# Layer 0 of a two-layer decoder trunk: tokens laid out by residue class, value projections as seven half-size products, blocks of the first attention group taken from the folded layout

## The chip, the cores and the metric

The kernel runs on one core of one Trainium2 chip. The metric is the device time of one execution in microseconds; the time of a kernel is the median of its runs. A core has a matrix engine (TensorE, in the profile PE, with its weight loads as PEld), two engines for elementwise work (VectorE, DVE; ScalarE, ACT), a general one (GpSimd, POOL), and a queue engine (SyncE, SP) that here only issues transfers. Each engine works through its own instructions in order and waits on semaphores for the others. Matrix products land in PSUM, of which this kernel uses eight banks of 128 x 512 float32; everything else lies in SBUF.

## What is computed

512 tokens of 1024 channels go through two layers. Layer 0 mixes tokens by attention in three groups of eight heads, layer 1 by trailing means; each is followed by a gated feed-forward block with 2816 hidden channels. Cut to what matters here:

```python
ATTN_PAIRS = ((128, 1), (512, 4), (2048, 16))     # window, dilation
qkv = (h @ w_qkv).reshape(B, S, 3, 3, 8, 128)      # group, q/k/v, head, dim
for g, (window, dil) in enumerate(ATTN_PAIRS):
    # inside each of the dil residue classes: a causal band of width window/dil
    o_g, lse_g = dilated_window_attention(q, k, v, window, dil, slopes[g])
wts = softmax(stack(lses), axis=0)                 # over the three groups
x = x + (sum(wts * outs)) @ w_out
x = x + (silu(gate) * up) @ w_down                 # after RMSNorm
```

With 512 tokens, group 1 has four residue classes of 128 tokens each; group 2 is computed in the same four classes, with all pairs masked whose distance is not a multiple of 16. Group 0 has a band of 128 tokens and is computed in four blocks of 128 queries against the block itself and the one before.

## The kernel before

All large matrices are kept as sums of two float32r parts, a high and a low one: ScalarE copies a weight tile to its high part and VectorE subtracts (`split`, L77 to L79). A product of two such matrices is three matmuls: high by high, high by low, low by high.

*Two kinds of product.* `Product` (L217 to L251) gives 128 output channels for all 512 tokens from eight chunks of 128 input channels: 24 matmuls that stream 512 columns, all recorded on L245, L246 and L248. `seven` (L393 to L431) gives two such outputs at once in seven half-size products in place of eight: 84 matmuls that stream 256 columns (L384 to L386, in `mult`). It needs the weights in three combined forms and a plain quarter, which the class `Pair` makes: three loads on SP and one accumulating load on GpSimd (L134 to L138), two additions on VectorE (L150, L151), three splits of 128 x 1024 and one of 128 x 512. The token side is combined once, in `prepare` (L661), which writes the operands `T["11"]` to `T["4"]`. The results are put together by four VectorE additions out of PSUM (L420, L424, L429, L430).

*Order of work.* `units`, `loads` and `steps` are queues in the order in which products will ask for weights; `pump` starts the next loads and splits as buffers come free. There are five split tiles of 1024 columns (`w`), two of 512 (`half`), four raw tiles (`raw`) and two raw halves.

*Layer 0.* For each head the queries and keys of the three groups are made (for head 0 and 1 by `Product`, from head 2 on by three calls of `seven`). The values are made for two heads at a time: on even heads `values` (L496 to L522) makes those of group 0 for this head and the next, with the tokens as the stationary operand, in 96 matmuls of 256 columns (L509 to L511); on odd heads `values12` (L473 to L494) makes those of groups 1 and 2 in 96 matmuls of 512 columns (L484 to L486) whose stationary operand is read with a stride of four tokens (`H[k]` rearranged by `fold`, L482), and ScalarE copies the four results out (L493).

*Layout.* Tokens are kept in their natural order. Groups 1 and 2 want them by residue class, so their queries and keys are written in class order when they leave PSUM: `Folded` (L361) for `seven`, L469 for the single products; L650 reads and writes the output through a stride of four.

*Attention of a head.* `scores0` (L530) makes the scores of group 0, `scores12` (L564) those of groups 1 and 2. A row's maximum and sum for group 0 lie in block order, those for groups 1 and 2 in class order, so each pair is sent through DRAM to the other order: `dn` (L560, L561) and `df` (L587, L588), all four issued on SP. `merge` (L591) combines maxima and sums and scales the scores, `turn` (L611) transposes them on TensorE, `output` (L629) multiplies them by the values. `between` (L737) and the dictionaries given to `values` and `values12` say after which product each of these steps is written for each head; the scheduler then orders the instructions of each engine by priority and readiness. `halve` splits a head's output into two parts for the output projection; the last steps of head 7 stand in L788 to L802.

*Start.* Five matmuls on zeros run first (`WARM`, L707), then four products with the chunks as they arrive (L709 to L724), a fifth (L725), the row factors of the norm (`rstd`, L726; `spread`, L731) amid a sixth.

Of the kernel before, what the change touches and what calls it, by code (L numbers as in the profile page):

```python
# [16 lines left out]
P = 128  # L17
S = 512
# [8 lines left out]
NT = S // P  # L27
FAR = 3.0e38
# [8 lines left out]
WARM = 5  # L37
# [11 lines left out]
def trunk(ctx: ExitStack, tc: tile.TileContext, xT, norms, w_first, w_qk, w_qkp, w_v0, w_v12, w_out, w_pair, w_down, w_pin, w_pgrp,  # L49
# [72 lines left out]
    class Pair:  # L122
# [3 lines left out]
        def __init__(self, src):  # L126
            self.src, self.w = src, {}
            loads.append((self, {"raw": 2, "rawhalf": 1}, self.load))
            steps.extend([(self, "w", self.blocks), (self, "w", self.sums), (self, "w", self.more),
                          (self, "half", self.last)])  # L130
# [43 lines left out]

    def plain_gu(layer, j):
        src = w_pair[layer, j]
        units.extend([Plain(src[:, S:3 * S]), Plain(src[:, 3 * S:], src[:, :S])])
# [4 lines left out]
    for h in range(HEADS):  # L182
        if h == 0:
            plain(*[w_qk[u] for u in range(len(QK) - NF)])
        for g in range(3):
            if h == 1 and g < NSOLO:
                plain(*[w_qk[len(QK) - NF + 2 * g + c] for c in range(2)])
            elif h:
                units.append(Pair(w_qkp[3 * h - 3 - NSOLO + g]))
        if h % 2 == 0:  # L190
            plain(*[w_v0[h // 2, i] for i in range(2)])
        else:
            plain(*[w_v12[h // 2, i] for i in range(4)])
    plain(*[w_out[m] for m in range(KC)])

    def ffn_plan(layer):
        for hf in range(2):
            for j in range(hf * HALF, (hf + 1) * HALF):
                if j < NPLAIN:
                    plain_gu(layer, j)  # L200
                else:
                    units.append(Pair(w_pair[layer, j]))
# [141 lines left out]
    class Straight:  # L344


        @staticmethod
        def both(t):
            return t.rearrange("p (a c) -> p a c", a=2)

        @classmethod
        def one(cls, t, a):
            return cls.both(t)[:, a]

        scratch = out = both

        @staticmethod
        def twice(v):
            return v[:, None].to_broadcast([P, 2, H2])

    class Folded(Straight):  # L361


        @staticmethod
        def both(t):
            return t.rearrange("p (a i r) -> p a r i", a=2, r=NT)

        @staticmethod
        def scratch(t):
            return t.rearrange("p (a r i) -> p a r i", a=2, r=NT)  # L370

        @staticmethod
        def out(t):
            return t.rearrange("p (r a i) -> p a r i", a=2, r=NT)

        @staticmethod
        def twice(v):
            return v[:, None].to_broadcast([P, 2, NT, H2 // NT])

# [13 lines left out]
    def seven(T, one, two, scratch, view=Straight, after={}):  # L393


        unit = units.popleft()
# [10 lines left out]
        nc.scalar.copy(view.scratch(first)[:, 0], view.one(p1, 0))  # L407
# [12 lines left out]
        nc.vector.tensor_add(view.out(one), view.both(p26), view.twice(view.scratch(first)[:, 0]))  # L420
# [3 lines left out]
        nc.vector.tensor_add(view.scratch(sums), view.both(p73), view.twice(view.out(one)[:, 1]))  # L424
# [4 lines left out]
        nc.vector.tensor_sub(view.out(two), view.both(p45), view.twice(view.scratch(sums)[:, 0]))  # L429
        nc.vector.tensor_sub(view.out(one)[:, 1], view.scratch(sums)[:, 1], view.one(p45, 1))  # L430
# [19 lines left out]
    fold = "p (i r) -> p r i"  # L450
    unfold = "p (r i) -> p r i"


    with tc.tile_pool(name="opool", bufs=1) as opool:
        early = opool.tile([P, HEADS, S], F32R, tag="o", name="early")
        with tc.tile_pool(name="apool", bufs=1) as apool:
# [5 lines left out]

            def evac(h, u, p):
                g, c = QK[u]
                t = apool.tile([P, S], F32, name=f"qk{g}{c}")
                if g == 0:
                    nc.vector.tensor_mul(t, p, rows["row"])
                else:
                    nc.vector.tensor_mul(t.rearrange(unfold, r=4), p.rearrange(fold, r=4),  # L469
                                         rows["row"].rearrange(fold, r=4))  # L470
                QKV[h, g, c] = t

            def values12(after={}):  # L473
# [3 lines left out]
                ps4 = [ps() for b in range(NT)]  # L477
                for k in range(KC):
                    if k % 2 == 0:
                        w = weights()  # L480
                    wh, wl = (v[:, k % 2 * S:(k % 2 + 1) * S] for v in w.t)
                    oph, opl = (v.rearrange(fold, r=4) for v in H[k])  # L482
                    for b in range(NT):
                        nc.tensor.matmul(ps4[b], oph[:, b, :], wh, start=k == 0, stop=False)  # L484
                        nc.tensor.matmul(ps4[b], oph[:, b, :], wl, start=False, stop=False)  # L485
                        nc.tensor.matmul(ps4[b], opl[:, b, :], wh, start=False, stop=k == KC - 1)  # L486
                    if k % 2:
                        w.done()
                    pump()
                    for f in after.get(k, ()):  # L490
                        f()
                for b in range(NT):
                    nc.scalar.activation(t[:, b, :], ps4[b], AF.Copy)  # L493
                return t  # L494

            def values(of, r=None, after={}):  # L496


                w = weights(), weights()
                t = apool.tile([P, NT, 2 * P], F32, name="v0")  # L500
                for b in range(NT):
                    if b % 2 == 0:
                        p = ps()
                    o = blk(p, b % 2 * 2, 2)
                    for k in range(KC):
                        c = slice(k % 4 * 2 * P, (k % 4 + 1) * 2 * P)
                        wh, wl = (v[:, c] for v in w[k // 4].t)
                        mh, ml = (blk(v, b) for v in of(k))
                        nc.tensor.matmul(o, mh, wh, start=k == 0, stop=False)  # L509
                        nc.tensor.matmul(o, mh, wl, start=False, stop=False)  # L510
                        nc.tensor.matmul(o, ml, wh, start=False, stop=k == KC - 1)  # L511
                    if b % 2:
                        for a in (b - 1, b):
                            nc.scalar.activation(t[:, a, :], blk(p, a % 2 * 2, 2), AF.Copy,
                                                 scale=r[:, a:a + 1] if r is not None else 1.0)
                    pump()
                    for f in after.get(b, ()):
                        f()
                for v in w:
                    v.done()  # L520
                pump(2)
                return t  # L522
# [7 lines left out]
            def scores0(h):  # L530
# [28 lines left out]
                with nc.allow_non_contiguous_dma(reason="a few numbers a token"):  # L559
                    nc.sync.dma_start(dn.rearrange("s (b p) -> p s b", p=P), st[:, 0, 0])  # L560
                    nc.sync.dma_start(st[:, 1, 1], dn.rearrange("s (i r) -> i s r", r=4))  # L561
                A[h] = dict(b12=b12, st=st, nm=nm, s0=s0)

            def scores12(h):  # L564
# [21 lines left out]
                with nc.allow_non_contiguous_dma(reason="a few numbers a token"):  # L586
                    nc.sync.dma_start(df.rearrange("s (i r) -> i s r", r=4), st[:, 0, 1])  # L587
                    nc.sync.dma_start(st[:, 1, 0], df.rearrange("s (b p) -> p s b", p=P))  # L588
                A[h]["s12"] = s12

            def merge(h):  # L591
# [6 lines left out]
                nc.vector.tensor_max(mx, st[:, 0, :, 0, :], st[:, 1, :, 0, :])  # L598
# [30 lines left out]
            def output(h):  # L629
# [13 lines left out]
                nc.scalar.copy(o0, po)  # L643
# [457 lines left out]
```

## Time and profile before

| | |
|---|---|
| median of three runs | 1275.57 us (1275.15 to 1278.36) |
| the profiled execution | 1277.5 us, of which the span of instructions is 1275.7 us |
| TensorE busy | 1262.7 us, 99% of the span |
| VectorE busy | 866.3 us, 68% |
| ScalarE busy | 529.4 us, 41% |
| GpSimd busy | 106.4 us, 8% |
| read from HBM | 160.40 MB, 127 GB/s over the span |

Layer 0's attention lies in the first 517 us of the span, layer 0's feed-forward block from there to about 868 us, the trailing means of layer 1 up to about 930 us, and its feed-forward block after that. How to read the views: a group of instructions is given as line, engine, operation, written tile and read tiles, how many there are, their busy time and the mean of one, and what ended the idle time before them. A matmul's recorded duration contains its way through the array, which overlaps the next one; what a matmul costs in a stream is the distance from its start to the next start. A window is a stretch of the span with the busy time of each engine in it and, in brackets, the number of instructions.

### The profile page before, as it was taken

To read this page: it belongs to the slowest core of one execution; us is meant where nothing else is said; L and a number is where in the kernel's file an instruction comes from. 1 tells how busy PE (TensorE), PEld (TensorE's weight loads), DVE (VectorE), ACT (ScalarE), POOL (GpSimd) and SP (SyncE) were. 2 spreads that over 40 slices of the span, in tenths; PEclk is the share of its full clock that TensorE was granted. 3 is DMA by queue.
4 is the path that set the end of the run, shared out by engine and by line. 5 is a ranking of instruction groups with operands and counts; after the bars stand their busy time and mean duration, and the time that the engine had idled before them with its cause. 6 is when DMAs were issued, how large, how long until landed. Compare 5 with 4: busy or idle time off the path is not lost.

```text
span 1275.7 us, 20125 instructions
## 1 busy us (share of the span) xinstructions
PE 1262.7 (99%) x8036; PEld 1165.3 (91%) x8036; DVE 866.3 (68%) x1313; ACT 529.4 (41%) x825; POOL 106.4 (8%) x105
## 2 busy tenths in 40 slices
PE   9999999999999999999999999999999999999997
PEld 7989999999999998889989999888788988999986
DVE  6794876658566637578636887458978853788643
ACT  6443444444344424445324454333443532455331
POOL 1101101010110100001001110000300000111000
PEclk9999999999999999999999999999999999999999
DMA  8143546446644713147346774333124645676222
GB/s 292 52 142 75 149 133 137 124 110 159 119 117 134 179 53 124 58 100 183 121 141 156 187 180 126 108 139 116 50 67 111 173 139 132 173 182 170 95 69 66
DMA packets 83454, 163.88 MB, mean 128 GB/s; under 512 B 27440, under 2 KB 29504, under 8 KB 83360
## 3 DMA queue, kind: packets, MB, share of 16 engines
q1 hardware_dynamic: 67792, 132.82, 33.4%
q0 software_dynamic: 14416, 28.72, 13.5%
q8 instruction: 63, 1.03, 0.3%
q10 hardware_dynamic: 1152, 1.05, 0.2%
q14 instruction: 31, 0.25, 0.1%
HBM read 160.40 MB, written 2.16 MB: 127 GB/s over the span
## 4 chain that ended last, share of the span: by engine, by line
PE 80%; issue 10%; DVE 6%; DMA 2%; ACT 1%; POOL 1%; SPq 0%; DVEq 0%; POOLq 0%; ACTq 0%
PE ps L385 12%; PE ps L384 12%; PE ps L386 12%; PE ps L245 9%; PE ps L248 9%; PE ps L246 9%; PE ps L484 2%; PE ps L485 2%; PE ps L486 2%; DVE wlo L79 2%; PE ps L647 1%; PE ps L510 1%; PE ps L509 1%; PE ps L511 1%; PE ps L573 1%
## 5 line engine op out<-in xcount | busy, mean ns | idle before, releaser
L79 DVE TENSOR_TENSOR wlo<-raw,whi 128x1024 fp32r<-128x1024 f32 (+2 forms) x286 | 327.0, 1146 | 199.9 <-ACT whi L78 198.8
L78 ACT ACTIVATE whi<-raw 128x1024 fp32r<-128x1024 f32 (+2 forms) x286 | 283.9, 998 | 420.8 <-PE ps L246 203.0
L245 PE MATMUL ps<-a,whi 128*128 128x512 f32 (+1 forms) x374 | 141.0, 377 | 0.0
L246 PE MATMUL ps<-a,whi 128*128 128x512 f32 (+1 forms) x374 | 140.9, 377 | 0.0
L248 PE MATMUL ps<-a,wlo 128*128 128x512 f32 (+1 forms) x374 | 140.8, 377 | 0.0
L384 PE MATMUL ps<-tt,whi 128*128 128x256 f32 x384 | 108.7, 283 | 0.0
L385 PE MATMUL ps<-tt,whi 128*128 128x256 f32 x384 | 108.7, 283 | 0.0
L386 PE MATMUL ps<-tt,wlo 128*128 128x256 f32 x384 | 108.7, 283 | 0.0
L248 PEld LDWEIGHTS ps<-a,wlo 128*128 128x128 f32 x374 | 70.4, 188 | 12.9
L246 PEld LDWEIGHTS ps<-a,whi 128*128 128x128 f32 x374 | 70.4, 188 | 12.8
L245 PEld LDWEIGHTS ps<-a,whi 128*128 128x128 f32 x374 | 70.4, 188 | 12.7
L137 POOL DMA_DIRECT2D raw<-w_pair x32 | 38.3, 1197 | 445.7 <-DVE wlo L79 168.2
L384 PEld LDWEIGHTS ps<-tt,whi 128*128 128x128 f32 x384 | 73.7, 192 | 0.0
L385 PEld LDWEIGHTS ps<-tt,whi 128*128 128x128 f32 x384 | 73.7, 192 | 0.0
L386 PEld LDWEIGHTS ps<-tt,wlo 128*128 128x128 f32 x384 | 73.7, 192 | 0.0
L385 PE MATMUL ps<-tb,whi 128*128 128x256 f32 x256 | 72.6, 284 | 0.5 <-DVE tb L79 0.5
L386 PE MATMUL ps<-tb,wlo 128*128 128x256 f32 x256 | 72.4, 283 | 0.0
L384 PE MATMUL ps<-tb,whi 128*128 128x256 f32 x256 | 72.4, 283 | 0.0
L245 PE MATMUL ps<-h,whi 128*128 128x512 f32 x160 | 62.7, 392 | 0.0
L248 PE MATMUL ps<-h,wlo 128*128 128x512 f32 x160 | 62.3, 389 | 0.0
L246 PE MATMUL ps<-h,whi 128*128 128x512 f32 x160 | 62.3, 389 | 0.0
L384 PE MATMUL ps<-h,whi 128*128 128x256 f32 x216 | 61.9, 286 | 0.0
(247 smaller groups left out, 3329.7 us busy)
## 6 DMA issues: line engine op xcount, KB each, us to landing
raw<-w_pair SPq DMA_DIRECT2D x76, 512.0 KB, 4.2
raw<-w_qkp SPq DMA_DIRECT2D x36, 512.0 KB, 4.7
raw<-w_pair POOLq DMA_DIRECT2D x32, 512.0 KB, 7.1
raw<-w_v SPq DMA_DIRECT2D x24, 512.0 KB, 3.5
raw<-w_down SPq DMA_DIRECT2D x32, 384.0 KB, 3.1
raw<-w_down SPq DMA_DIRECT2D x32, 320.0 KB, 2.8
raw<-w_qkp POOLq DMA_DIRECT2D x18, 512.0 KB, 7.3
rawhalf<-w_pair SPq DMA_DIRECT2D x32, 256.0 KB, 3.3
```

The lines of the kernel that those rows point to most:

```text
L78: nc.scalar.activation(hi, v, AF.Copy)
L79: nc.vector.tensor_tensor(lo, v, hi.bitcast(F32), op=OP.subtract)
L137: nc.gpsimd.dma_start(self.b.t.rearrange("p (a c) -> p a c", a=2), self.src[:, None, 3 * S:].to_broadcast([P, 2, S]), accum_op=OP.add)
L245: nc.tensor.matmul(self.p[:, cols], w[0][:, s], mh[:, cols], start=self.done == 0, stop=False)
L246: nc.tensor.matmul(self.p[:, cols], w[0][:, s], ml[:, cols], start=False, stop=False)
L248: nc.tensor.matmul(self.p[:, cols], w[1][:, s], mh[:, cols], start=False, stop=self.done == self.n)
L384: nc.tensor.matmul(dst, w.t[0][:, c], th, start=k == 0, stop=False)
L385: nc.tensor.matmul(dst, w.t[0][:, c], tl, start=False, stop=False)
L386: nc.tensor.matmul(dst, w.t[1][:, c], th, start=False, stop=k == K2 - 1)
L484: nc.tensor.matmul(ps4[b], oph[:, b, :], wh, start=k == 0, stop=False)
L485: nc.tensor.matmul(ps4[b], oph[:, b, :], wl, start=False, stop=False)
L486: nc.tensor.matmul(ps4[b], opl[:, b, :], wh, start=False, stop=k == KC - 1)
```

## The change

The tokens of layer 0 are sent in by residue class from the host: position (r, i, b) of the new order is token 128 b + 4 i + r. A class of 128 tokens is then contiguous, and a block of 128 tokens is every fourth position. The change has these parts:

- `values12` becomes seven half-size products with the tokens as the stationary operand, each over two classes: 7 x 2 x 4 x 3 = 168 matmuls of 256 columns. Its weights come as two `Pair`s whose steps alternate (`pairs`). The results are put together by seven VectorE operations; the four ScalarE copies of L493 go, one ScalarE copy of the first product comes.
- The values of group 0 are made like queries and keys, with the channels on the partitions: for head 0 by two `Product`s, for heads 2, 4 and 6 by `seven` with a `Pair`; the new `turn_values` transposes them, eight transposes and two ScalarE copies for two heads, for heads 2, 4 and 6 after the next head's first `seven`.
- `Straight` and `Folded` go. Groups 1 and 2 are written as they come. Group 0's queries, keys and values are written by blocks (`by_block`): four neighbouring positions of the source go to four places 128 columns apart. `output` writes its first half through a stride of four (`block`) and adds the second without one.
- `merge` is tied by `issue_after` to the last result (`mark`) of the latest `seven` or `values12`, and moves: for odd heads h-1 it is written after the next head's first `seven`, for even ones after the second, for head 7 after `values12`. `scores0` and `turn` move with it; `scores12` goes to the first of the seven products. The two exchanges through DRAM change sides: `dn` is now written in pieces of four numbers and read in single ones, `df` written in single ones and read in fours.
- The identity and the two distance tables are loaded on SP after the first sixteen loads, not on GpSimd at the start. There are six matmuls on zeros. The fifth product is written after the first `prepare`, and all four `prepare` calls come within head 0.
- At the end of layer 0's feed-forward block `unfold` adds the last projection to the stream and writes the sum in the natural order into another tile; one ScalarE copy moves the first of these tiles back.

```diff
-WARM = 5
+WARM = 6
...
+    def by_block(t):
+        return t.rearrange("p (b a j) -> p a j b", a=2, b=NT)
+    def by_class(t):
+        return t.rearrange("p (a j b) -> p a j b", a=2, b=NT)
...
-        nc.vector.tensor_add(view.out(one), view.both(p26), view.twice(view.scratch(first)[:, 0]))
+        nc.vector.tensor_add(into(one), out(p26), again(out(first)[:, 0]))
...
-        nc.vector.tensor_sub(view.out(one)[:, 1], view.scratch(sums)[:, 1], view.one(p45, 1))
+        mark.append(nc.vector.tensor_sub(into(one)[:, 1], out(sums)[:, 1], out(p45)[:, 1]))
...
             def values12(after={}):
...
+                    for a in range(2):
+                        for k in range(K2):
+                            wh, wl = (v[:, half * S + k % 2 * H2:half * S + (k % 2 + 1) * H2]
+                                      for v in part(unit[k // 2], name).t)
+                            mh, ml = (blk(v, a) for v in T[key, k])
+                            o = both(p)[:, a]
+                            nc.tensor.matmul(o, mh, wh, start=k == 0, stop=False)
+                            nc.tensor.matmul(o, mh, wl, start=False, stop=False)
+                            nc.tensor.matmul(o, ml, wh, start=False, stop=k == K2 - 1)
...
+            def turn_values(h):
+                t = apool.tile([P, NT, 2 * P], F32, name="v0")
+                for c in range(2):
+                    p = ps()
+                    for b in range(NT):
+                        nc.tensor.transpose(blk(p, b), blk(VT[c], b), ident)
+                    nc.scalar.copy(t[:, :, c * P:(c + 1) * P], p.rearrange("p (b d) -> p b d", b=NT))
...
-                    nc.sync.dma_start(dn.rearrange("s (b p) -> p s b", p=P), st[:, 0, 0])
-                    nc.sync.dma_start(st[:, 1, 1], dn.rearrange("s (i r) -> i s r", r=4))
+                    nc.sync.dma_start(dn.rearrange("s (p b) -> p s b", b=NT), st[:, 0, 0])
+                    nc.sync.dma_start(st[:, 1, 1], dn.rearrange("s (r p) -> p s r", r=NT))
...
-                nc.vector.tensor_max(mx, st[:, 0, :, 0, :], st[:, 1, :, 0, :])
+                with tc.issue_after(mark[-1].ins) if mark else nullcontext():
+                    nc.vector.tensor_max(mx, st[:, 0, :, 0, :], st[:, 1, :, 0, :])
...
                 if h % 2:
-                    if h == 1:
-                        return {0: [], 1: [later(merge, 0)], 2: [later(turn, 0), later(scores0, 1)]}[g]
-                    return {0: [later(merge, h - 1)], 1: [later(turn, h - 1), later(scores0, h)], 2: []}[g]
-                return {0: [later(output, h - 2), later(turn, h - 1)], 1: [later(output, h - 1), later(scores0, h)],
-                        2: []}[g]
+                    return {0: [later(turn_values, h - 1)] if h > 1 else [], 1: [later(merge, h - 1)],
+                            2: [later(turn, h - 1), later(scores0, h)] + [later(scores12, h)] * (h == HEADS - 1)}[g]
+                return {0: [later(merge, h - 1), later(output, h - 2)], 1: [later(turn, h - 1), later(scores0, h)],
+                        2: [later(output, h - 1)]}[g]
...
+        def unfold(m, p):
+            if m == 0:
+                held["x", 0], t = slot("xs", F32)
+                new = t[:, 0]
+            else:
+                new = x_tile(m - 1)
+            nc.vector.tensor_add(new.rearrange("p (b i r) -> p r i b", r=NT, b=NT), *(
+                t.rearrange("p (r i b) -> p r i b", r=NT, b=NT) for t in (X[m], p)))
+            X[m] = new
```

252 lines of the change are left out of this document (132 added, 120 removed).

## The prediction

> **What bounds the kernel now.** I read the page's totals first, then what TensorE waited for, then windows over one pair of heads.
>
> ```profile
> span 1275.7 us, 20125 instructions
> PE 1262.7 (99%) x8036; PEld 1165.3 (91%) x8036; DVE 866.3 (68%) x1313; ACT 529.4 (41%) x825; POOL 106.4 (8%) x105
> ```
>
> TensorE is busy for 99% of the span. Its waits, from the longest to the last listed:
>
> ```profile
> PE ps L322 <- POOL rcol L314: 1.3, 2, 1.1
> ...
> PE ps L618 <- DVE s L606: 0.2, 1, 0.2
> ```
>
> The whole list has eight entries and none is above 1.3 us, so no other engine holds TensorE up: only fewer or cheaper matmuls shorten the span, and only a new wait of TensorE lengthens it. Two pairs of heads, and a stretch of the feed-forward block that holds nothing but half-size products (columns: window, its length, then busy time and instructions of PE, PEld, DVE, ACT and POOL, granted clock, DMA share, GB/s):
>
> ```profile
> 147.62:259.05 111.43, 111.43 (x835) 111.03 (x835) 73.67 (x118) 45.74 (x84) 12.56 (x13) 1.00 0.52 132
> 259.05:370.49 111.44, 111.44 (x836) 111.05 (x835) 73.16 (x118) 45.56 (x84) 12.33 (x13) 1.00 0.58 129
> 710.00:750.00 40.00, 40.00 (x336) 40.00 (x335) 34.55 (x48) 20.96 (x28) 4.61 (x4) 1.00 0.74 183
> ```
>
> A pair of heads costs 111.4 us, all of it TensorE; VectorE works for 66% of that. The third row gives the price of a 256-column matmul, 40.00 / 336 = 0.119 us, and shows TensorE unhindered beside a VectorE that is 34.55 / 40.00 = 86% busy. The granted clock is full throughout.
>
> **The change part by part.** *`values12`.* The old call for head 3, from its first matmul to the first of the next product:
>
> ```profile
> 205.73 0.51 PE L484 MATMUL ps<-whi,h 128*128 128x512 f32 x1
> ...
> 211.49 1.95 PE L573 MATMUL ps<-qk,qk 128*128 128x128 f32 x16
> 213.19 0.60 PE L484 MATMUL ps<-whi,h 128*128 128x512 f32 x1
> ...
> 230.42 0.28 PE L384 MATMUL ps<-h,whi 128*128 128x256 f32 x1
> 230.54 0.28 PE L385 MATMUL ps<-h,whi 128*128 128x256 f32 x1
> ```
>
> From 205.73 to 230.42 are 24.69 us; 213.19 - 211.49 = 1.70 of them are the scores of L573. So 96 matmuls cost 22.99 us, 0.239 each. The new call has 168 of 256 columns. The last two rows stand 0.12 apart, the window gave 0.119; at 0.1195 the call costs 20.1 and saves 2.9 us, four calls 11.6. This does not ask why the old call paid 0.239; the stride of its stationary tiles is only the likeliest reason. The Trainium skill ("TensorE: Matmul & The Clock Gate", section "Back-to-back issue gap") lists 518 cycles for 512 columns and 262 for 256 at 2.4 GHz, by which I estimate 96 x 0.216 = 20.7 us before and 168 x 0.109 = 18.3 after: 2.4 saved a call, 9.6 in four, or 2.0 less than by the rows. No stream of either width here is that fast, so the rows stand.
>
> *`values`.* The eight transposes of `turn_values` are priced by the eight of `turn`:
>
> ```profile
> 133.28 0.87 PE ps L624 x8
> ```
>
> For heads 2, 4 and 6, 96 matmuls become 84: 12 x 0.1195 = 1.43 saved, 0.87 paid, 0.56 left, 1.7 in three. For head 0 they become 48 of 512 columns, at the distance of these rows:
>
> ```profile
> 42.45 0.39 PE L246 MATMUL ps<-early,whi 128*128 128x512 f32 x1
> 42.68 0.39 PE L248 MATMUL ps<-early,wlo 128*128 128x512 f32 x1
> 42.91 0.28 PE L509 MATMUL ps<-whi,early 128*128 128x256 f32 x1
> 43.02 0.28 PE L510 MATMUL ps<-wlo,early 128*128 128x256 f32 x1
> ```
>
> 48 x 0.23 + 0.87 - 96 x 0.1195 = 0.4 us lost.
>
> *The sixth matmul on zeros.*
>
> ```profile
> 1.24 4.63 PE L708 MATMUL ps<-idle 128*128 128x256 f32 x10 [1.24 <-DVE idle L705]
> 6.41 0.79 PE L245 MATMUL ps<-early,whi 128*128 128x512 f32 x1 [0.54 <-ACT whi L718]
> ...
> 9.99 0.55 PE L248 MATMUL ps<-early,wlo 128*128 128x512 f32 x1
> 10.38 0.39 PE L245 MATMUL ps<-early,whi 128*128 128x512 f32 x1
> 10.61 0.40 PE L246 MATMUL ps<-early,whi 128*128 128x512 f32 x1
> ```
>
> One more is 4.63 / 5 = 0.93 us; 0.54 of it fits into the wait for the first weights, so the loss is 0.4, at most 0.9. Matmuls of 512 columns stand 0.39 apart until 10.38 and 0.23 after it. Should that switch come earlier by as much as TensorE starts earlier, up to 1.6 would be gained. I take the loss of 0.4.
>
> *VectorE.* The rows of its work (out and in shapes, count, busy time and mean ns, idle time before):
>
> ```profile
> L79 DVE TENSOR_TENSOR wlo<-raw,whi 128x1024 fp32r<-128x1024 f32 x222 | 270.3, 1220 | 131.4 <-ACT whi L78 131.0
> L150 DVE TENSOR_TENSOR raw<-raw 128x512 f32<-128x512 f32 x50 | 34.2, 684 | 16.7 <-issue 16.4
> L420 DVE TENSOR_TENSOR qk<-ps,first 128x512 f32<-128x512 f32 x18 | 12.3, 683 | 0.0
> L430 DVE TENSOR_TENSOR qk<-sums,ps 128x256 f32<-128x256 f32 x18 | 7.4, 409 | 0.0
> L467 DVE TENSOR_TENSOR qk<-ps,row 128x512 f32<-128x512 f32 x4 | 2.6, 680 | 1.1 <-ACT row L731 1.1
> L469 DVE TENSOR_TENSOR qk<-ps,row 128x512 f32<-128x512 f32 x8 | 8.3, 1068 | 0.0
> L650 DVE TENSOR_TENSOR o<-o,ps 128x512 f32<-128x512 f32 x8 | 8.9, 1107 | 14.9 <-PE ps L647 14.9
> ```
>
> A `Pair` takes 3 x 1.22 + 3 x 0.68 = 5.7 us (two additions, one half split). For `values12` two of them replace four plain splits: 11.4 - 4.9 = 6.5 more, and seven results of 0.68 add 4.8. For `values` one replaces two splits, 3.3 more, and four results add 3 x 0.68 + 0.41 = 2.5. L650 without its stride gives back 2 x 0.4. That is 16.3 a pair of heads. Writing by blocks is new. L469 reads the row factors from SBUF, and its product from PSUM, through a stride: 0.39 over L467. L420 read PSUM through the same stride at 683, so the dearer part is SBUF. L650 also writes through one and costs only 0.04 more than L469. So a block-wise write lies between nothing and 0.4 us; over the results of three products, 3 x 3.5 full-size operations, at most 4.2 a pair. I take 2. VectorE then has 73.7 + 16.3 + 2 = 92.0 us in 111.4 - 2.9 - 0.6 = 107.9, or 85%, no more than the 86% beside which TensorE ran unhindered above. Without that cover each microsecond over would count in full. ScalarE, at 46 of 111 us, loses four copies and gets five smaller jobs; it is nowhere near.
>
> *Order and transfers.* `merge` waits on VectorE for both exchanges; behind it stand splits, behind those TensorE.
>
> ```profile
> 218.06 0.49 ACT L584 ACTIVATE s<-s,nm 128x256 f32<-128x256 f32 x1
> ...
> 227.39 0.17 DVE L598 TENSOR_TENSOR mx<-st 128x8 f32<-128x8 f32 x1 [5.74 <-DMA st<-df]
> ```
> ```profile
> DVE mx L598 <- DMA st<-df: 26.9, 7, 10.4
> ```
> ```profile
> dn<-st SPq DMA_DIRECT2D x8, 4.0 KB, 10.3
> st<-dn SPq DMA_DIRECT2D x8, 4.0 KB, 3.5
> df<-st SPq DMA_DIRECT2D x8, 4.0 KB, 4.3
> st<-df SPq DMA_DIRECT2D x8, 4.0 KB, 2.8
> ```
>
> The new `df` is written in single numbers, as `dn` was: 10.3 + 3.5 = 13.8 us. For an odd head h-1 it starts after the values' first product (84 / 7 = 12 matmuls, 1.4 us) or, after `values12`, its first 24 (2.9 us), and the scores: these began at 211.49 and their last exponential ended at 218.55, 7.1 us. So for an even head h, whose `values` runs, it lands near 1.4 + 7.1 + 13.8 = 22.3; for an odd head near 23.8. The new `merge` waits for the next head's first result (odd: 20.1 + 1.7 + 10.0 = 31.8) or for an even head's successor's second (later still). So it finds its data some 8 us old, and VectorE's 26.9 us of waiting should go; TensorE did not notice them, so I book nothing. SP, too, works in order, and its read of `df` cannot start before those 10.3 us are over, so the weight loads issued after it start so much later. What hides that are tiles already split: five in the ring, each good for 24 matmuls or 2.9 us, 14.3 us when full. Four raw tiles lie ahead of these. I book nothing, and at most 0.5 a head, 3.5 in seven.
>
> *Moved loads and the start.* The identity and the two tables leave GpSimd for SP, behind the first sixteen loads and ahead of the weights:
>
> ```profile
> 11.90 2.19 SPq L114 DMA_DIRECT2D raw<-w_qk x2
> ...
> 36.81 1.04 POOL L314 TENSOR_TENSOR rcol<-var,nhalf 128x4 f32<-128x4 f32 x1 [28.75 <-DVE var L312]
> ```
>
> SP issues these weights 1.1 us apart, so three loads push them back by some 3 us, while TensorE is fed from the first sixteen; and the identity is asked for only after the row factor at 36.81, some 20 us past its landing. GpSimd, which builds the bias tables from the two distance tables, has 28.75 us idle to do it in. Nothing for this; were TensorE to ask for those weights at once, the 3 us would count, but the four lead products, 96 matmuls, come first.
>
> *Head 0.* Here VectorE is the tight engine:
>
> ```profile
> 48.66:92.88 44.22, 44.01 (x234) 37.51 (x233) 39.48 (x70) 23.24 (x45) 4.47 (x5) 1.00 0.30 89
> ```
>
> It is busy for 39.48 / 44.22 = 89% already. Two `prepare` calls move ahead of this stretch's splits, the two value tiles are written by blocks, and `turn_values` asks for the second as soon as the product is done, with only the scores' 1.7 us between them. I book 1.0 (0 to 2.5), and 0.5 (0 to 1.5) for TensorE's other waits on a result within the pairs.
>
> *The tail.* `merge` of head 7 now follows `values12`; ahead of the transposes that need it TensorE has 18 matmuls of 512 columns, 18 x 0.23 = 4.1 us, and `output` of head 6. I book nothing; what is left over falls under the other waits above. `unfold` makes eight additions with a stride on both sides, by L650 against L903 at most 0.4 us dearer each:
>
> ```profile
> L903 DVE TENSOR_TENSOR x<-x,ps 128x512 f32<-128x512 f32 x30 | 20.6, 686 | 44.2 <-PE ps L248 44.2
> ```
>
> VectorE waited 44.2 us for TensorE at this line, which hides them; uncovered they would be 3.
>
> *The sum.* -11.6 - 1.7 + 0.4 + 0.4 + 1.0 + 0.5 = -11.0, so a span of 1264.7. The profiled execution took 1277.5, 1.8 over its span and 1.9 over the median of the runs: 1264.7 + 1.8 - 1.9 = 1264.6.
>
> **The rivals.** *Head 0 stalls.* The two `prepare` calls stand ahead of the splits of head 1's weights. Were all of the stage's free VectorE time, 44.22 - 39.48 = 4.7 us, to come as a wait instead, the end would be at 1264.6 + 4.7 = 1269. For it: the 89%. Against it: TensorE was busy for 44.01 of the 44.22 beside that load.
>
> *Block-wise writes are dear.* VectorE has 107.9 - 90.0 = 17.9 us left a pair before such writes; from 17.9 / 10.5 = 1.7 us more each it is the bound, and at 2.0 more a pair takes its old 111 us: near 1275, no change. Against it: no stride in the rows costs more than 0.42. The Trainium skill ("SBUF — State Buffer", the row "Cachelines" of its table) says that each step to another 16-byte line pays; by that the 16-byte stride of L469 pays at every element as a longer one would, and the price stays near 0.4. The trace bears it out as far as L467 and L469 go; no row of it has the longer stride.
>
> *Slower: VectorE stands still at `merge`.* Tied to a result, with `df` now the slow exchange and its read behind weight loads on SP, `merge` can keep the splits waiting as long as the longest wait before, 10.4 us. Of five split tiles one is being read and one written, and beside a VectorE at 85% half the ring, 7.2 us, is a fair cover: 3.2 us a head, seven heads, 22: 1287. It decides from 7.2 + 11 / 7 = 8.8 us a head. For it: the 10.4 itself. Against it: the 8 us of margin above.
>
> *It does not do what it says.* With tokens as the stationary operand and weights streaming, 256 columns could cost more than 0.1195. At 22.99 / 168 = 0.137 the main term is gone: 1264.6 + 11.6 = 1276. Against it: L509 and L510 above are of that kind, and stand 0.11 apart.
>
> **How the numbers follow.** Forecast 0.60, head 0 0.15, dear writes 0.09, `merge` 0.14, the last 0.02. The forecast's own range: the warm-up's bounds (-2.0 to +0.5 about its term), those of `turn_values` (-1.0 to +1.5) and of the other waits (-0.5 to +1.0) give 1261.1 to 1267.6 if all fall to one side. The range takes in head 0 and the edge of the third case, 1260 to 1275.5, and leaves out `merge`. A measurement tells 0.3%, 3.8 us, from no change: the first two cases are faster, 0.75; dear writes and the last are the same, 0.11; `merge` is slower, 0.14.
>
> **What would show it.** Right: matmuls of the new `values12` 0.12 apart, a call of 20 us without its scores, a pair of heads near 108 us, VectorE near 85% in it, next to no time in front of L598's successor, block-wise results at 0.7 to 1.1 us. Wrong: TensorE's waits on split tiles inside the pairs; a wait of several microseconds at `merge`; block-wise results above 2 us; a gap in front of the transposes of head 0.

## The result and the profile after

| | before | changed |
|---|---|---|
| median | 1276.70 us (10 runs, 1275.15 to 1284.85) | 1289.99 us (10 runs, 1285.53 to 1300.50) |
| ratio | | 1.0107, 95% interval 1.0080 to 1.0134 |
| profiled execution | 1277.5 us, span 1275.7 | 1300.5 us, span 1298.7 |

The change makes the kernel 1.1% slower; 1264.6 was forecast, and 1275.5 was the upper end of the range. The profiled execution of the changed kernel is the longest of its ten, 10.5 us above their median, so its waits are read for where they lie, and sizes are taken from the medians of runs. The loss lies in the attention of layer 0: VectorE's first addition of the output projection starts at 501.4 us in the profile, at 477.1 before, and what follows takes 797.3 us of span against 798.6.

The totals of the changed kernel's page:

```profile
PE 1261.7 (97%) x8274; PEld 1157.6 (89%) x8274; DVE 930.1 (72%) x1398; ACT 542.4 (42%) x831; POOL 125.5 (10%) x113
```

TensorE is no longer busy all the time: it had 99% of the span and has 97%. The pair of heads from the scores of head 3 to those of head 5, of the changed kernel, with the columns of the windows shown before:

```profile
205.50:324.83 119.33, 112.29 (x905) 110.06 (x903) 91.04 (x143) 48.76 (x86) 18.00 (x15) 0.98 0.58 140
```

A pair took 111.43 us, should have taken 107.9, and takes 119.33. VectorE has 91.04 us of work in it, where 92.0 were forecast: the load is right, the time is not. Of the 11.4 us over the forecast, 7.0 are time in which TensorE stands idle; the other 4.4 are longer busy time, at a mean granted clock of 0.98 (third number from the right). What TensorE waits for in the changed kernel (total, times, longest):

```profile
PE ps L640 <- DVE s L628: 12.4, 6, 3.3
PE ps L256 <- ACT oh L79: 5.7, 1, 5.7
PE ps L569 <- DVE qk L414: 5.1, 4, 1.5
```

L640 is the first transposition of `turn`, L628 the multiplications in `merge`; L569 is the second half of `scores0`, which waits for L414, the first result of a `seven` that VectorE reads out of PSUM, presumably for its bank; L256 is the output projection, waiting for the last heads' halves at the end of the attention. Only the first was in the list before, with 0.2 us. `merge` itself, however, no longer waits for its transfers. VectorE's waits of the changed kernel:

```profile
DVE raw L152 <- issue: 39.0, 11, 4.8
...
DVE mx L620 <- DMA st<-df: 0.6, 1, 0.6
```

The 26.9 us in front of `merge` (now L620) are down to 0.6, as forecast. Grown is L152, the first addition that makes the third form of a `Pair`'s weights (L150 before): 39.0 us in eleven waits against 16.4 in five. Between 92 and 500 us, in the attention, it is 25.1 us in six waits, one ahead of each `merge` of heads 1 to 6, against 1.4 in one before; most of the rest lies in the feed-forward blocks, where the kernel before had it too. One of the six, on VectorE of the changed kernel, ahead of the `merge` of head 4:

```profile
306.49 0.68 DVE L414 TENSOR_TENSOR qk<-ps,first 128x512 f32<-128x512 f32 x1
311.50 0.69 DVE L152 TENSOR_TENSOR raw<-raw 128x512 f32<-128x512 f32 x1 [4.33 <-issue]
312.11 0.68 DVE L418 TENSOR_TENSOR sums<-ps,qk 128x512 f32<-128x512 f32 x1
315.37 1.23 DVE L80 TENSOR_TENSOR wlo<-raw,whi 128x1024 fp32r<-128x1024 f32 x1 [2.58 <-ACT whi L79]
316.51 0.68 DVE L423 TENSOR_TENSOR qk<-ps,sums 128x512 f32<-128x512 f32 x1
317.12 0.41 DVE L424 TENSOR_TENSOR qk<-sums,ps 128x256 f32<-128x256 f32 x1
317.44 0.16 DVE L620 TENSOR_TENSOR mx<-st 128x8 f32<-128x8 f32 x1
...
321.57 1.07 DVE L628 TENSOR_SCALAR s<-s,co 128x256 f32<-128x256 f32 x4
```

and what TensorE and GpSimd did at that time:

```profile
308.44 0.28 PE L374 MATMUL ps<-h,whi 128*128 128x256 f32 x1
...
321.98 1.35 PE L640 MATMUL ps<-ident,s 128*128 128x128 f32 x7 [3.30 <-DVE s L628]
```
```profile
300.82 1.24 POOL L139 DMA_DIRECT2D raw<-w_v  x1 [17.17 <-DVE qk L424]
```

TensorE ended the `seven` whose results these are at 308.44, where the next one starts. VectorE, which works in order, has L152 ahead of the second result; L152 reads a raw tile to which GpSimd's accumulating load of 300.82 adds a quarter; that load landed 10.6 us after its issue, at 311.42, and L152 starts at 311.50. Then a split waits another 2.58. The last result, the one that `merge` is tied to, ends at 317.53, 9.1 us after TensorE was done; `merge` starts at 317.44, its first multiplications, with steps on weights in between, at 321.57, and `turn`, which TensorE reaches one product later, waits 3.30 us for them.

### The profile page after: what moved, and what is told of

It is laid out like the page before. It is cut to its first block, busy times and chain, and to the rows that moved or that the text cites. A ratio compares the mean times of both kernels' runs of the same rounds, so it can differ in the third digit from the quotient of the medians.

```text
span 1298.7 us, 20811 instructions
## 1 busy us (share of the span) xinstructions
PE 1261.7 (97%) x8274; PEld 1157.6 (89%) x8274; DVE 930.1 (72%) x1398; ACT 542.4 (42%) x831; POOL 125.5 (10%) x113
## 4 chain that ended last, share of the span: by engine, by line
PE 68%; issue 12%; DVE 10%; DMA 7%; ACT 1%; POOL 1%; SPq 0%; DVEq 0%; POOLq 0%; ACTq 0%
PE ps L256 10%; PE ps L257 10%; PE ps L374 10%; PE ps L259 10%; PE ps L375 10%; PE ps L376 10%; DMA raw<-w_qkp 3%; DVE wlo L80 2%; DMA df<-st 2%; DMA raw<-w_v 1%; PE ps L594 1%; DMA raw<-w_out 1%; ACT whi L79 1%; PE ps L669 1%; POOL rcol L325 1%
## 5 line engine op out<-in xcount | busy, mean ns | idle before, releaser
L79 ACT ACTIVATE whi<-raw 128x1024 fp32r<-128x1024 f32 (+2 forms) x297 | 294.1, 1000 | 472.1 <-PE ps L257 195.5
L80 DVE TENSOR_TENSOR wlo<-raw,whi 128x1024 fp32r<-128x1024 f32 (+2 forms) x297 | 340.3, 1150 | 176.9 <-ACT whi L79 173.7
L256 PE MATMUL ps<-a,whi 128*128 128x512 f32 (+1 forms) x374 | 141.0, 377 | 0.0
L257 PEld LDWEIGHTS ps<-a,whi 128*128 128x128 f32 x374 | 70.4, 188 | 12.8
L256 PEld LDWEIGHTS ps<-a,whi 128*128 128x128 f32 x374 | 70.4, 188 | 12.8
L374 PE MATMUL ps<-h,whi 128*128 128x256 f32 x252 | 74.0, 294 | 0.8 <-DVE sums L418 0.8
L375 PE MATMUL ps<-h,whi 128*128 128x256 f32 x252 | 72.6, 288 | 0.0
L376 PE MATMUL ps<-h,wlo 128*128 128x256 f32 x252 | 72.6, 288 | 0.0
L152 DVE TENSOR_TENSOR raw<-raw 128x512 f32<-128x512 f32 x61 | 41.8, 685 | 39.3 <-issue 39.0
```

Source lines behind the costliest of these rows:

```text
L79: nc.scalar.activation(hi, v, AF.Copy)
L80: nc.vector.tensor_tensor(lo, v, hi.bitcast(F32), op=OP.subtract)
L152: nc.vector.tensor_add(a[:, :S], a[:, :S], b[:, :S])
L256: nc.tensor.matmul(self.p[:, cols], w[0][:, s], mh[:, cols], start=self.done == 0, stop=False)
L257: nc.tensor.matmul(self.p[:, cols], w[0][:, s], ml[:, cols], start=False, stop=False)
L374: nc.tensor.matmul(dst, w.t[0][:, c], th, start=k == 0, stop=False)
```

## Experiments

Theory A, formed from the above: the loads of the values' new `Pair`s come late, VectorE stands at L152, the results and the `merge` tied to them stand behind it, and TensorE runs into `turn` and `scores0`. Theory B: one product between the last result and `turn` is too short for `merge`, loads or no loads. Medians are given with the ratio to the kernel before on the same chip, whose own median drifted from 1277.8 to 1280.7 us between the sets. Kernels are therefore compared by ratio, from 1.0107 for the changed kernel, and a hundredth stands for 12.8 us.

### The exchange, the pin and the place of `merge`

Faster `df` (e1):

```diff
-nc.sync.dma_start(df.rearrange("s (r p) -> p s r", r=NT), st[:, 0, 1])
-nc.sync.dma_start(st[:, 1, 0], df.rearrange("s (p b) -> p s b", b=NT))
+nc.sync.dma_start(df.rearrange("s (p r) -> p s r", r=NT), st[:, 0, 1])
+[nc.sync.dma_start(st[r * NI:(r + 1) * NI, 1, 0, s], df.rearrange("s (j b r) -> s r j b", b=NT, r=NT)[s, r])
+ for s in range(2) for r in range(NT)]
```

> Only the exchange df differs: written in runs of four numbers, read in single ones by eight small reads (L608, L609); the order of instructions on VectorE and TensorE stays that of the changed kernel. Theory A (the slow write keeps SP at the read of df for 11.5 us a head, the loads of the next pair of weights start late, VectorE stands at the addition L152 with the results and merge behind it): SP's wait at L609 falls from 92.0 us to under 45, VectorE's at L152 from 39.0 to under 20, TensorE's at L640 from 12.4 to under 4 and at L256 for oh from 5.7 to under 1; time 1264 to 1272. Theory B (one product between the last result and turn is too short for merge, whatever the loads do): L640 stays at 9 or more, time 1283 to 1290.

Measured: 1279.75 us, ratio 1.0017 (0.9999 to 1.0036). SP's waits of the changed kernel and then of e1:

```profile
SPq L609 <- DMA df<-st: 92.0, 8, 13.7
```
```profile
SPq L609 <- DMA df<-st: 40.2, 8, 7.7
```

and, in e1, VectorE's at the addition and TensorE's at `turn`:

```profile
DVE raw L152 <- issue: 41.4, 11, 5.3
```
```profile
PE ps L640 <- DVE s L628: 6.4, 4, 2.1
```

0.0090 are gained, some 11 us, and the wait at `turn` is halved, but neither theory is met: L152 stands as long as before. That doesn't clear SP's stand at `df`, for SP is hardly free sooner in e1. SP's rows for head 4, of the changed kernel and then of e1:

```profile
283.40 0.38 SPq L608 DMA_DIRECT2D df<-st  x1
294.54 0.38 SPq L609 DMA_DIRECT2D st<-df  x1
295.02 1.67 SPq L136 DMA_DIRECT2D raw<-w_v  x1
```
```profile
278.47 0.38 SPq L608 DMA_DIRECT2D df<-st  x1
286.07 6.21 SPq L609 DMA_DIRECT2D st<-df  x8
292.39 0.52 SPq L136 DMA_DIRECT2D raw<-w_v  x1
```

The write lands sooner, but the eight small reads take SP 6.2 us to issue. From the issue of the write to the next load of weights pass 11.6 us in the changed kernel and 13.9 in e1 here, and 13.1 and 12.4 on the mean of heads 0 to 6. So e1 does not test what it was made for, and where its 11 us come from stays open.

No pin (e2), and no pin with the faster `df` (e3):

```diff
-with tc.issue_after(mark[-1].ins) if mark else nullcontext():
+if True:
     nc.vector.tensor_max(mx, st[:, 0, :, 0, :], st[:, 1, :, 0, :])
```

> issue_after is taken away, merge may stand in VectorE's queue ahead of the results; nothing else. Theory A: the late loads stay, so the waits at L569 for the results (5.1 us) and the tail's 5.7 stay and only those at L640 shrink: 1277 to 1284. Theory B: the waits of TensorE at L640 go with the pin, 1268 to 1276. If VectorE standing at merge for the exchange were the cost that the pin avoids, slower than the changed kernel: over 1292.

> The faster exchange df and no pin. Without the pin VectorE stood 68.6 us at merge for the exchange in twelve and more microseconds each; with 8 us less a head about 15 are left. If this stand is all that the pin avoids: 1268 to 1276, level with or better than the pin. If the order of the queue itself is bad: over 1282.

Measured: 1308.89 us, ratio 1.0238 (1.0209 to 1.0268), and 1281.63, 1.0014 (0.9988 to 1.0040). The scheduler now puts `merge` ahead of results, and VectorE waits there, in e2 and then in e3:

```profile
DVE mx L620 <- DMA st<-df: 68.6, 8, 11.5
```
```profile
DVE mx L620 <- DMA st<-df: 20.7, 6, 6.4
```

In e2 VectorE stands at `merge` as in the slower rival of the prediction, which the pin avoids in the changed kernel. With the faster exchange the pin no longer matters: e3, whose time lies between the two that were expected, and e1 are alike. And yet e2 and e3 have no more than 0.3 us at L152 between 92 and 500 us, where the changed kernel has 25.1 and e1 26.5. So the stand at the addition is not the only one that costs: without it VectorE stands elsewhere in front of results, and TensorE waits 7.3 us at L569 in e3.

`merge` one product earlier (e4), and both this and the faster `df` (e5):

```diff
 # odd h
-0: [later(turn_values, h - 1)] if h > 1 else [], 1: [later(merge, h - 1)],
+0: ([later(turn_values, h - 1)] if h > 1 else []) + [later(merge, h - 1)], 1: [],
 # even h
-0: [later(merge, h - 1), later(output, h - 2)],
+0: [later(output, h - 2)],
 # odd h, h < 7
-values12({0: [later(scores12, h)]})
+values12({0: [later(scores12, h)], 6: [later(merge, h)]})
```

> merge is written one product earlier for every head but the last (for odd heads after values12, for even ones after the next head's first seven), the pin stays. Theory A: L640 falls under 4 us, the waits for results at L569 and the tail stay: 1276 to 1283. Theory B: nearly all of the loss goes, 1266 to 1273.

> Both edits, the faster df and merge one product earlier. Theory A: no better than the faster df alone within 3 us, 1263 to 1271. Theory B: as merge earlier alone, 1266 to 1273. If each cures a part of its own, 1262 to 1267, clearly below either.

Measured: 1283.60 us, 1.0029 (1.0010 to 1.0049), and 1270.51, 0.9935 (0.9911 to 0.9958). In e4 `turn` is off the list, and the other waits have grown:

```profile
PE ps L256 <- ACT oh L79: 9.2, 1, 9.2
PE ps L569 <- DVE qk L414: 7.1, 4, 2.8
```

Merge earlier gains 0.0078, the faster exchange 0.0090, both 0.0172: each cures a part of its own, and together they beat the kernel before, though not down to the 1262 to 1267 us expected of that. B explains its part, but not all. The order matters for L152 too: between 92 and 500 us its waits are 5.3 us in e4 and 5.4 in e5.

### The values' pairs

`values12` as it was, on the new layout (e6):

```diff
-pairs(w_v12[h // 2, 0], w_v12[h // 2, 1])
+plain(*[w_v12[h // 2, i] for i in range(4)])
...
+oph, opl = H[k]
+for b in range(NT):
+    nc.tensor.matmul(ps4[b], blk(oph, b), wh, start=k == 0, stop=False)
...
```

> The changed kernel with values12 as it was: four plain split tiles a call, 96 matmuls of 512 columns, four copies on ScalarE; the tokens stay by residue class, so the stationary tiles are contiguous. On TensorE 96 x 0.227 = 21.8 us a call in place of 20.1, 6.6 more in four calls, if the stride was what made 22.99; 22.99 and 11.5 more if it was not. Theory A in its present form (VectorE stands at L152 for the accumulating load of a pair, and two pairs at once for values12 fill the four raw tiles, so that loads start late): the waits at L152 in front of merge shrink for the even heads' stages, L640 falls under 8, time 1284 to 1290, the matmuls' loss nearly balanced. If pairs for values12 have no part in the waits: 1296 or more.

Measured: 1268.98 us, 0.9922 (0.9891 to 0.9952), 0.0185 or 24 us less than the changed kernel, though TensorE has more to do. I had expected the matmuls' loss to be nearly balanced. The window of e6 from the scores of head 3 to those of head 5:

```profile
200.56:310.33 109.77, 109.77 (x832) 105.66 (x831) 80.76 (x127) 48.98 (x85) 14.72 (x13) 1.00 0.57 138
```

TensorE is never idle in it. VectorE at the same place as in the section above:

```profile
296.66 0.68 DVE L414 TENSOR_TENSOR qk<-ps,first 128x512 f32<-128x512 f32 x1
297.45 0.69 DVE L418 TENSOR_TENSOR sums<-ps,qk 128x512 f32<-128x512 f32 x1
298.40 1.22 DVE L80 TENSOR_TENSOR wlo<-raw,whi 128x1024 fp32r<-128x1024 f32 x1 [0.26 <-ACT whi L79]
...
300.14 0.41 DVE L424 TENSOR_TENSOR qk<-sums,ps 128x256 f32<-128x256 f32 x1
300.47 0.16 DVE L580 TENSOR_TENSOR mx<-st 128x8 f32<-128x8 f32 x1
```

No addition stands between the results. The last of them ends at 300.55, 1.9 us after TensorE ended the product (298.62), where it was 9.1 in the changed kernel; `merge` starts at 300.47 and its multiplications at 302.45, 2.0 us later in place of 4.1. The slow exchange, the pin and the late place of `merge` are all still there in e6, and so is SP's stand at the exchange (L569 of e6):

```profile
SPq L569 <- DMA df<-st: 79.7, 8, 11.6
```

The other way round, e8 makes the two edits of e5 on e6:

> values12 plain, the faster df, and merge one product earlier. If the slow exchange and the late merge cost nothing by themselves and only turned the pairs' late loads into waits of TensorE: the same as values12 plain alone, 1267 to 1271, though these two edits took 19.5 us off the changed kernel. If they cost something of their own: under 1265.

Measured: 1270.35 us, 0.9924 (0.9895 to 0.9953), the same as e6. The two edits that were worth 0.0172 beside the pairs are worth nothing without them. In e8 VectorE even stands 16.8 us at `merge` for the exchange, and TensorE waits for nothing of it.

What about the pairs costs so much? They bring VectorE work, a load chain (a load on SP, then an accumulating one on GpSimd into the same tile), and they hold all four raw tiles, since two pairs of two are under way at once. And `values12` in seven products has its results put together on VectorE, in order with everything else there, where e6 has ScalarE copy them. VectorE's work alone, added to e6 (e11):

```diff
+spin = scratch("first")
+nc.vector.memset(spin, 0.0)
 for k in range(KC):
+    for i in range(2):
+        nc.vector.tensor_add(spin, spin, spin)
```

> values12 plain with four raw tiles, and sixteen additions of 128 x 512 on a spare tile in each call (16 x 0.68 = 10.9 us), about the work that the two pairs and the seven results add on VectorE (11.3 us). If VectorE's load is what the pairs cost: 1280 or more, with TensorE waiting for VectorE. If it is the loads and the order of the queue: within 4 us of 1269.

Measured: 1271.11 us, 0.9926 (0.9902 to 0.9951). The same pair of heads in e11:

```profile
201.93:311.69 109.76, 109.76 (x832) 105.67 (x831) 90.63 (x144) 48.74 (x85) 13.52 (x13) 1.00 0.57 136
```

VectorE is as loaded as in the changed kernel, 90.63 us against 91.04, and TensorE does not feel it. These additions wait for nothing, so e11 clears the work, not the order in which the seven results stand.

The accumulating load left out for the values' weights of the changed kernel (e9):

```diff
-nc.gpsimd.dma_start(self.b.t.rearrange("p (a c) -> p a c", a=2),
-                    self.src[:, None, 3 * S:].to_broadcast([P, 2, S]), accum_op=OP.add)
+if self.add:
+    nc.gpsimd.dma_start(...)
```

> The changed kernel without the accumulating loads of GpSimd for the weights of the values (11 of 61): one quarter of those weights is left out of the sums, so the values differ; matmuls and VectorE's work are the same. If it is this load that VectorE waits for at L152 ahead of results and merge: L152's 39.0 us fall under 20, TensorE's waits at L640 from 12.4 to under 5, time 1276 to 1283. If it is the first loads on SP or the ring of raw tiles: L152 stays over 30 and the time within 4 us of 1290.

Measured: 1280.92 us, 1.0014 (0.9992 to 1.0036). That gains 0.0093, 12 us. The addition's wait (one line further down in e9) falls, and `turn` is off TensorE's list, though its wait at the output projection is 7.8 us (5.7 in the changed kernel):

```profile
DVE raw L153 <- issue: 25.9, 7, 4.4
```

It was expected under 20. Between 92 and 500 us, where the values' weights are loaded, it fell from 25.1 to 9.7; the rest lies in the feed-forward blocks, whose loads are as before.

Late loads without pairs for `values12`: e6 with three raw tiles in place of four (e10).

```diff
-BUFS = {"w": 5, "half": 2, "raw": 4, "rawhalf": 2}
+BUFS = {"w": 5, "half": 2, "raw": 3, "rawhalf": 2}
```

> values12 plain again (1268.98 us with four raw tiles), and now three raw tiles in place of four, so that weights are loaded later while matmuls and VectorE's work stay. If late loads are what makes VectorE stand at L152 in front of results and merge: TensorE's waits at the transposes and for results come back, several us in sum, time over 1276. If the kernel has loads to spare: within 3 us of 1269.

Measured: 1296.55 us, 1.0138 (1.0104 to 1.0173). This holds for the whole kernel; the pair of heads in e10 shows the attention's part:

```profile
202.50:320.20 117.70, 113.38 (x833) 108.21 (x832) 82.44 (x131) 47.69 (x85) 13.24 (x13) 0.97 0.54 132
```

117.70 in place of 109.77: one raw tile less costs a pair of heads 7.9 us, with the same matmuls and hardly more work on VectorE (82.44 us against 80.76). But the waits at the transposes that were expected did not come back: in this window TensorE waits 3.0 us for a result at L414 and 1.3 for others. So a shortage of raw tiles costs time, but not at the transposes, where the changed kernel waits most. The opposite, a fifth raw tile for the changed kernel, was not tried.

### The start

Five matmuls on zeros in place of six, on e5 (e7) and on e6 (e12).

```diff
-WARM = 6
+WARM = 5
```

> Faster df, merge one product earlier, and five matmuls on zeros in place of six. If the sixth brings the full granted clock to the first real matmuls: 1.5 to 2.5 slower than with six, 1272 to 1273, and the first products' matmuls 0.39 apart until about 10 us. If it only costs its own length: 0.5 faster, 1270.

> values12 plain with five matmuls on zeros. If the sixth brings the full clock forward: 1 to 2 us slower than 1268.98; if it costs 0.4: 1268.5.

Measured: 1268.98 us, 0.9916 (0.9886 to 0.9947) against 0.9935 with six, and 1270.90, 0.9919 (0.9891 to 0.9948) against 0.9922. The sixth matmul can't be told from nothing in either.

## Why the prediction was wrong

*The step that failed* is the one on order and transfers, which booked nothing for `merge` and the late loads. It put the new `merge` at "20.1 + 1.7 + 10.0 = 31.8", the moment at which TensorE ends the product, and took the results as there at once. They stand in VectorE's queue, and there L152 came first: the last was 9.1 us late in the stretch shown. The same step asked of late weights only whether TensorE would run out of split tiles ("What hides that are tiles already split"). No wait for weights is among TensorE's waits of the changed kernel; what ran late was what stood behind the weights in VectorE's queue: results, `merge`, and through them, it seems, PSUM banks. That `merge` has only one more product's time, 10 us, to be done before `turn` was nowhere priced. "0.5 (0 to 1.5) for TensorE's other waits on a result within the pairs" is the term that was to hold all this. The measured time is 25.4 us above the forecast; e6 against the changed kernel puts what `values12` in seven products brings along at 24 us, and 7 more for the matmuls that e6 pays besides. Some 5 us of these 31 were gained elsewhere against the forecast, which was not traced.

*The term for `values12`* had its matmuls right and lacked its weights. The new call of head 3 on TensorE:

```profile
207.61 0.36 PE L484 MATMUL ps<-whi,h 128*128 128x256 f32 x1
...
210.57 1.95 PE L594 MATMUL ps<-qk,qk 128*128 128x128 f32 x16
212.27 0.36 PE L484 MATMUL ps<-whi,h 128*128 128x256 f32 x1
...
229.63 0.28 PE L374 MATMUL ps<-h,whi 128*128 128x256 f32 x1
```

22.02 us less 1.70 for the scores are 20.3, or 0.121 a matmul; 20.1 was forecast, and the rival of matmuls at 0.137 falls. By the rule of the Trainium skill ("TensorE: Matmul & The Clock Gate", section "Back-to-back issue gap") I had estimated 18.3; the trace does not reach it. Of the 2.7 saved a call, the layout alone brings a part: the 96 matmuls of 512 columns of e6's call for head 3 take 21.99 us without its scores, from 202.00 to 225.69, where the same 96 took 22.99 before. So the stride of the old stationary tiles cost about 1.0 us a call, and the seven products add some 1.7 to that, 7 in four calls. For these 7 us the kernel takes on the load chain.

*VectorE's load* was priced well (92.0 against 91.04) and, as e11 shows, was rightly put down as harmless by itself. *Head 0* did not stall: between 36 and 92 us TensorE's list of the changed kernel has no wait. The rows of block-written results in the changed kernel:

```profile
L414 DVE TENSOR_TENSOR vt<-ps,first 128x512 f32<-128x512 f32 x3 | 3.3, 1101 | 0.0
...
L423 DVE TENSOR_TENSOR vt<-ps,sums 128x512 f32<-128x512 f32 x3 | 3.2, 1080 | 0.0
```

At 1.08 to 1.10 us they are 0.4 over the 0.68 of a plain one, the upper bound; with the longer stride, of 512 bytes, the trace agrees with what the Trainium skill ("SBUF — State Buffer", the row "Cachelines") made of it, and the rival of dear writes falls.

*The slower rival* had nearly the measured time, 1287, and that is luck. `merge` waited 0.6 us for the exchange in all, where the rival put 3.2 a head; with the pin taken away, in e2, VectorE does stand there, 68.6 us, and the time is 1308.89. *Smaller terms:* for the start, 0.4 lost was booked, and the first real matmul came earlier than before (5.75 against 6.41), with the shorter distance, 0.23, from the second on:

```profile
5.75 0.58 PE L256 MATMUL ps<-early,whi 128*128 128x512 f32 x1
6.16 0.39 PE L257 MATMUL ps<-early,whi 128*128 128x512 f32 x1
6.39 0.40 PE L256 MATMUL ps<-early,whi 128*128 128x512 f32 x1
```

but e7 and e12 don't separate that from noise. The transfers had the right sides: the changed kernel's `dn` took 3.8 us and `df` 12.6, where 4.3 and 10.3 had been read from the rows before.

```profile
dn<-st SPq DMA_DIRECT2D x8, 4.0 KB, 3.8
st<-dn SPq DMA_DIRECT2D x8, 4.0 KB, 4.7
df<-st SPq DMA_DIRECT2D x8, 4.0 KB, 12.6
st<-df SPq DMA_DIRECT2D x8, 4.0 KB, 2.2
```

*What stays open:* how the loss divides between the accumulating load (0.0093 went with it in e9), the shortage of raw tiles (e10 shows a shortage at work in another kernel and without the waits at the transposes, not its share in this one), the seven results that now stand in VectorE's queue (no run keeps the pairs and takes the results elsewhere), and the exchange of `df`, whose faster write is worth 0.0090 in e1 without shortening the wait at L152 and with SP free hardly sooner. That `values12` in seven products, with all it brings, is the common condition of the last one and of the late `merge` is shown by e6 and e8; which part of it makes the exchange cost was not traced.

The fastest kernels, not told apart by their intervals, are e6 and its variants e8, e11 and e12, which keep the change but for the seven products of `values12`, and e5 with e7: 0.9916 to 0.9935 of the time before.

## What to carry to other kernels

When a step adds loads or preparations to an engine that works in order, don't compare its busy time alone: list what stands behind each of its waits, and how long the bound engine can do without that. A step that is tied to a result comes when the queue delivers the result, not when the product ends; leave it the time of the whole queue before its reader. When an edit is to free a queue sooner, look at when its next work starts: in e1 a wait fell by half and the issue of more transfers took its place. And a saving on the bound engine that is paid for with more buffers under way can take the slack that other waits were living on: the exchange and the late `merge`, harmless in e6, cost 0.0172 beside the pairs.

## What the runs showed besides

*Two of TensorE's waits cost more than their length.* Three waits in front of the transposes of the changed kernel, of 2.07, 3.30 (shown above, at 321.98) and 2.42 us,

```profile
139.80 1.04 PE L640 MATMUL ps<-ident,s 128*128 128x128 f32 x7 [2.07 <-DVE s L628]
...
440.80 1.13 PE L640 MATMUL ps<-ident,s 128*128 128x128 f32 x7 [2.42 <-DVE s L628]
```

and the windows that hold them or, for the second, follow it:

```profile
134.00:146.00 12.00, 8.10 (x58) 6.83 (x57) 11.90 (x27) 5.95 (x10) 1.20 (x1) 1.00 0.58 143
321.90:325.90 4.00, 3.92 (x18) 3.46 (x19) 4.00 (x11) 1.10 (x3) 0.52 (x1) 0.61 0.42 147
438.00:446.00 8.00, 5.58 (x28) 4.46 (x27) 7.96 (x19) 3.82 (x6) 0.00 (x0) 0.79 0.45 157
```

The granted clock (third number from the right) stays 1.00 with the first and falls with the two longer ones, to 0.61 and 0.79 over the window. The Trainium skill ("TensorE: Matmul & The Clock Gate", section "What's actually happening") has the clock halved after an idle window of about 3.4 us at no fixed phase. The first wait agrees with it; the other two are shorter than that, the second by little and the third by 1.0 us, and lost clock all the same. So here 3.4 us was no safe bound.

*Writing single numbers to DRAM was dear here, reading them less so.* `df` written in single ones took 12.6 us and `dn` in fours 3.8, while the reads in single ones (`st<-dn`) took 4.7 and those in fours 2.2; turned round in e1, `df` written in fours landed after 6.3 us and SP's wait for it fell from 92.0 to 40.2 us in eight heads, but its eight small reads took SP 0.6 us each to issue.
